# Ordering the expert-weight requests of a hybrid RWKV-7 / Mamba-2 / mixture-of-experts block by their use

## The chip, the cores and the metric

The kernel runs on one core of a Trainium2 chip. The metric is the device time of one execution in microseconds (us). Engines are named as in the profile: PE is TensorE (matmuls), PEld its weight loads, DVE VectorE, ACT ScalarE, POOL GpSimd, SP SyncE. SP does no arithmetic here. It issues DMA transfers, one after the other, and a request that has to wait holds up those behind it on SP.

## The reference, cut to what matters

One block with 512 tokens of 1024 channels in float32: two parallel mixers, an output projection, then a mixture of 32 experts, of which each token uses two. Only the last part is touched here.

```python
D_MODEL = 1024; SEQ = 512; N_GROUPS = 4; EXP_PER_GROUP = 8; N_EXPERTS = 32; TOP_K = 2; D_EXPERT = 512
def run_block(args):            # per expert e, on the tokens routed to it
    tok, e = args
    xb = ht[tok]
    hid = jax.nn.silu(xb @ w_gate[e]) * (xb @ w_up[e])
    return hid @ w_down[e]
...
y = jnp.zeros((T, D), f32).at[buf_tok].add(y_blocks.reshape(-1, D).astype(f32) * buf_w[:, None])
x = x + hier_moe(h2, ...)
return rmsnorm(x, final_norm_g)
```

## The kernel before

Mixers, projection and router fill the first two thirds of the time. Then comes the expert stage. The 32 experts are taken in 16 pairs, and each expert has 64 places for tokens (a loop behind the end handles more than 64; it isn't entered with these inputs). An expert's weights are three matrices of 2 MB (1 MB is 2^20 bytes here): gate, up and down. Each is loaded in two halves of 1 MB, one DMA request each, so a pair of experts takes 12 requests and the stage 192.

**Slots.** A request goes into one of 19 slots of 1 MB. They lie in four pools (tags `wa`, `we`, `wb`, `wc`), and `wslot` hands them out in a ring:

```python
NEXA, NEXB, NEXC, NEXD = 6, 8, 4, 1
def wslot(n, c):
    i = wcount[0] % (NEXA + NEXB + NEXC + NEXD)
    wcount[0] += 1
```

So the request with number r (from 0) waits until weight r - 19 was read for the last time. All requests are issued by SP (L954). A scheduler writes the order of SP, DVE, ACT and POOL, by the order of the program and by which slots it expects to be free; PE's order is that of the program.

**A pair on PE.** In iteration `j` of the main loop:

1. `hidden` for expert 2j: gate and up products, four of the eight 128-row slices of the contraction from the first halves of the weights (L1191, L1192).
2. In its middle, `first`: the hidden rows of pair j - 1 are transposed (`turn`, L1205), the older pair's results are partly added up (`combine`, L1243), and the pair's token selection is transposed (L1179).
3. The second halves of expert 2j's gate and up weights.
4. The scales and the gather's addresses for pair j + 1 (L1141; the gather itself runs on POOL, L1156).
5. `down_both` for pair j - 1 (L1230): the products with the down weights of both its experts.
6. `hidden` for expert 2j + 1, with `second` in its middle: `combine` and the transposes of the gathered tokens (`gather`, L1167).

After the loop come the down products of the last pair, one expert after the other (`down`, L1217), the last `combine`, a final RMS normalization with a gain that ACT loads (L1268, also into a slot of the ring), and the output's writes (L1334).

The down weights of pair j - 1 are thus read after half a pair of gate and up weights of pair j. They are requested, however, with the other weights of their expert: `expert_weights(e)` asks for gate 0, up 0, gate 1, up 1, down 0, down 1 (`WORD`), and is called ahead of each `hidden`.

Of the kernel before, what the change touches and what calls it, by code (L numbers as in the profile page):

```python
# [61 lines left out]
def hybrid_block(ctx: ExitStack, tc: tile.TileContext, a, out):  # L62
    nc = tc.nc
# [3 lines left out]
    def act(o, i, f, **kw):  # L67
        S.activation(o, i, f, **kw)  # L68
# [111 lines left out]
    with tc.tile_pool(name="first", bufs=1) as fp:  # L180
# [31 lines left out]
        for t in range(TT):  # L212
            n = (0, D, 0, D // 2)[t]
# [723 lines left out]
# [3 lines that stand above are left out]
        pool, tg, bf = ((exa, "wa", NEXA) if i < NEXA else (ex, "we", NEXB) if i < NEXA + NEXB else  # L940
                        (exb, "wb", NEXC) if i < NEXA + NEXB + NEXC else (exc, "wc", NEXD))
        return pool.tile([128, n, c], F32, name="we", tag=tg, bufs=bf)

    wsrc = [a["w_exp_gate"][0], a["w_exp_up"][0], a["w_exp_down"][0]]
    WDIM = [(KT, FE), (KT, FE), (4, D)]
    WORD = [(0, 0), (1, 0), (0, 1), (1, 1), (2, 0), (2, 1)]

    def expert_weights(e):
        ws = [[None, None] for j in range(3)]
        for j, i in WORD:  # L950
            n, c = WDIM[j]
            h2 = n // 2
            ws[j][i] = wslot(h2, c)
            nc.sync.dma_start(ws[j][i], wsrc[j][e].rearrange("(p k) f -> p k f", k=n)[:, h2 * i:h2 * i + h2])  # L954
        return ws

    X = mybir.AxisListType.X
    with tc.tile_pool(name="op", bufs=2, side="right") as op:
# [80 lines left out]
        def first(o, v, m, n):  # L1039
            tmp = sm(f"f{n}{o.name}", TT, n)  # L1040
            f = sm(f"g{n}{o.name}", TT)
            V.tensor_tensor(tmp, v, bcast(m, 2, n), op=OP.is_equal)
            V.tensor_tensor(tmp, tmp, bcast(jo[:, 0:n], 1, TT), op=OP.mult)
            V.tensor_reduce(f, tmp, axis=X, op=OP.min)
            V.tensor_tensor(o, bcast(jo[:, 0:n], 1, TT), bcast(f, 2, n), op=OP.is_equal)
# [137 lines left out]


    def hidden(xe, gsl, ws, e, between=lambda: None):
        wg, wu, wd = ws
        lo_, up_ = half[e], half[1 - e]
        pgu = eps_.tile([128, 512], F32, name="pgu", tag="pgu", bufs=2)
        for k in range(KT):
            x = xe[:, k, CAP * e:CAP * e + CAP]  # L1190
            PE.matmul(pgu[lo_], x, wg[k // 4][:, k % 4], start=k == 0, stop=k == KT - 1)  # L1191
            PE.matmul(pgu[up_], x, wu[k // 4][:, k % 4], start=k == 0, stop=k == KT - 1)  # L1192
            if k == KT // 2 - 1:
                between()
        if e == 0:
            hids[0] = mo.tile([128, FE], F32, name="hid", tag="hid")
        hid, g = hids[0], gsl[:, e:e + 1]
        act(hid[up_], pgu[lo_], AF.Silu, scale=g[lo_])
        V.scalar_tensor_tensor(hid[up_], pgu[up_], g[up_], hid[up_], op0=OP.mult, op1=OP.mult)

    def turn(hid, rows=slice(0, 128)):
        pt = eps_.tile([128, 4, 128], F32, name="pt", tag="pt", bufs=1)
        hk = hid.rearrange("p (c k) -> p c k", k=4)
        for k in range(4):
            PE.transpose(pt[:, k, rows], hk[rows, :, k], ident[rows, rows])  # L1205
        if hids[1] is None or rows.start == 0 and rows.stop == 128 or rows.start:
            hids[1] = mo.tile([128, 4, 128], F32, name="hT", tag="hT")
        V.tensor_copy(hids[1][:, :, rows], pt[:, :, rows])
        return hids[1]

    def down(hT, wd, yy, e):
        rows = half[e]
        tags = ("pgu", "pgu") if e == 0 else ("pd0", "pd1")
        pd = [eps_.tile([128, 512], F32, name=f"pd{i}", tag=tags[i], bufs=2 - e) for i in range(2)]
        for k in range(4):
            for i in range(2):
                PE.matmul(pd[i][half[i]], hT[:, k, half[1 - e]], wd[k // 2][:, k % 2, 512 * i:512 * i + 512],  # L1217
                          start=k == 0, stop=k == 3)
        for i in range(2):
            src = pd[i][half[i]]  # L1220
            act(yy[i][rows, 0], src, AF.Copy)
            V.tensor_tensor(yy[i][rows, 1], src, yy[i][rows, 0].bitcast(F32), op=OP.subtract)


    def down_both(hT, wds, yy):
        for i in range(2):
            pd = eps_.tile([128, 512], F32, name=f"pd{i}", tag=f"pd{i}", bufs=1)
            for k in range(4):
                for e in range(2):
                    PE.matmul(pd[half[e]], hT[:, k, half[1 - e]], wds[e][k // 2][:, k % 2, 512 * i:512 * i + 512],  # L1230
                              start=k == 0, stop=k == 3)
            act(yy[i][:, 0], pd, AF.Copy)
            V.tensor_tensor(yy[i][:, 1], pd, yy[i][:, 0].bitcast(F32), op=OP.subtract)

    def result_tiles():
        return [wp.tile([128, 2, 512], F32R, name="yy", tag="raw", bufs=2) for i in range(2)]

    def combine(oT, yy, n, ts=range(TT)):
        for t in ts:
            for i in range(2):  # L1240
                ps = ptile()
                for q in range(2):
                    PE.matmul(ps, oT[0:n, 128 * t:128 * t + 128], yy[i][0:n, q], start=q == 0, stop=q == 1)  # L1243
                av = x2[:, t, 512 * i:512 * i + 512]
                V.tensor_tensor(av, ps, av, op=OP.add)  # L1245
# [19 lines left out]
    def final_gain():  # L1265
        fng = wslot(2, D)[:, 0]
        fn_ = a["final_norm_g"]
        nc.scalar.dma_start(fng, bass.AP(tensor=fn_.tensor, offset=fn_.offset, ap=[[0, 128], [1, D]]))  # L1268
        return fng

    cur = Pair(0)
# [10 lines left out]
    before, older = None, None  # L1282
    NP = NE // 2
    for j in range(NP):
        last = j == NP - 1
        cur.ws = []


        def first():
            if before:  # L1290
                before.hT = turn(before.hid)
            if older:
                combine(older.oT, older.yy, 128, (2, 3))
            if j:
                cur.turned()

        def second():
            if last:
                cur.hT = turn(cur.hid, half[1])
            if before:  # L1300
                combine(before.oT, before.yy, 128, range(4) if last else (0, 1))
            if not last:
                nxt.gather()

        cur.ws.append(expert_weights(2 * j))
        hidden(cur.xe, cur.gsl, cur.ws[0], 0, first)
        cur.hid = hids[0]
        if before:
            if not last:
                nxt = Pair(j + 1)  # L1310
                nxt.scales()
                nxt.fetch()
            before.yy = result_tiles()
            down_both(before.hT, [w[2] for w in before.ws], before.yy)
        cur.ws.append(expert_weights(2 * j + 1))
        hidden(cur.xe, cur.gsl, cur.ws[1], 1, second)
        older, before, cur = before, cur, nxt
    fng = final_gain()
    before.yy = result_tiles()
    down(before.hT, before.ws[0][2], before.yy, 0)  # L1320
    turn(before.hid, half[0])
    down(before.hT, before.ws[1][2], before.yy, 1)

    def final_norm(fng, before=lambda t: None):
        ss = mo.tile([128, TT], F32, name="ss2", tag="ss2")
# [15 lines left out]
    with tc.If(most >= CAP + 1):  # L1341
        sx = mo.tile([128, CAP], F32, name="sx", tag="sx")
        V.tensor_scalar(sx, S0[:, 0], float(CAP), None, op0=OP.add)
        with tc.For_i(0, NE, 1) as e:
            ws = []
            for j in range(3):
                n, c = WDIM[j]
                h2 = n // 2
# [45 lines left out]
```

## Time and profile before

| | |
|---|---|
| runs | 1574.61, 1570.82, 1570.84 us; median 1570.84 |
| the profiled execution | 1568.6 us, of which 1566.9 us are the span that the profile covers |
| PE busy | 1442.3 us (92%) |
| DVE, ACT, POOL busy | 907.1, 662.8, 255.5 us |
| DMA | 325.31 MB, 208 GB/s over the span |
| expert weights | 192 requests of 1024 KB |

The shares are means over stages with different limits. In the expert stage PE and the DMA engines are both near full, so that only the waits and the distances between repeated steps tell which of them sets the pace. Times within the trace count from the span's start.

### The profile page before, as it was taken

How to read it: one execution, taken by the hardware profiler on the slowest of the kernel's cores; microseconds unless marked ns; L12 is line 12 of the kernel's file. 1: busy time of each engine (PE TensorE's matmuls, PEld its weight loads, DVE VectorE, ACT ScalarE, POOL GpSimd, SP SyncE). 2: the span in 40 equal slices, each digit the busy share in tenths (PEclk: the TensorE clock that was granted, in tenths of full speed). 3: DMA queues.
4: the chain of work that ended last, by engine and by line, in shares of the span. 5: the costliest groups of instructions: out<-in, count | busy, mean ns of one | idle time of the engine just before them, and what ended most of it. 6: DMA issues, size and time to landing. Idle time of an engine off the chain costs nothing. (4 is left out here: it accounts for less than half of the span.)

```text
span 1566.9 us, 21550 instructions
## 1 busy us (share of the span) xinstructions
PE 1442.3 (92%) x8066; PEld 933.8 (60%) x8066; DVE 907.1 (58%) x2066; ACT 662.8 (42%) x1278; POOL 255.5 (16%) x240
## 2 busy tenths in 40 slices
PE   6978999899998999989998988899999999999995
PEld 4655676567666777767686766784444344443432
DVE  4698767977778845454565576334444344443434
ACT  6556566566657544546554645321111111111111
POOL 3121002211122000142414355000000000000001
PEclk9998899999999999999999999999999999999998
DMA  4320222212222333774665437877799999999991
GB/s 143 86 66 26 56 85 77 61 57 62 76 63 82 110 94 115 232 210 146 178 187 164 152 101 235 271 283 288 298 419 425 424 424 423 423 424 426 424 419 72
DMA packets 189137, 325.31 MB, mean 208 GB/s; under 512 B 11977, under 2 KB 147395, under 8 KB 163427
## 3 DMA queue, kind: packets, MB, share of 16 engines
q1 hardware_dynamic: 180131, 316.90, 55.8%
q0 software_dynamic: 2304, 4.20, 0.8%
q10 hardware_dynamic: 6592, 2.77, 0.6%
q8 instruction: 66, 1.08, 0.3%
q14 instruction: 44, 0.36, 0.1%
HBM read 306.99 MB, written 21.04 MB: 209 GB/s over the span
## 5 line engine op out<-in xcount | busy, mean ns | idle before, releaser
L149 PE MATMUL pin<-hh,wh 128*128 128x512 f32 x664 | 296.9, 447 | 2.7 <-ACT wh L68 1.5
L151 PE MATMUL pin<-hh,wl 128*128 128x512 f32 x664 | 269.4, 406 | 7.2 <-DVE wl L134 7.2
L150 PE MATMUL pin<-hl,wh 128*128 128x512 f32 x664 | 268.9, 405 | 0.8 <-DVE hl L229 0.8
L1192 PE MATMUL pgu<-we,xe 128*64 128x512 f32 x512 | 233.1, 600 | 7.7 <-DMA we<-in_w_exp_up_dram 7.7
L1191 PE MATMUL pgu<-we,xe 128*64 128x512 f32 x512 | 233.3, 600 | 0.6 <-DMA we<-in_w_exp_gate_dram 0.6
L134 DVE TENSOR_TENSOR wl<-raw,wh 128x1024 fp32r<-128x1024 f32 x115 | 149.6, 1301 | 95.2 <-ACT wh L68 95.2
L68 ACT ACTIVATE wh<-raw 128x1024 fp32r<-128x1024 f32 x115 | 121.5, 1057 | 104.3 <-PE pin L150 84.5
L151 PEld LDWEIGHTS pin<-hh,wl 128*128 128x128 f32 x664 | 128.7, 194 | 41.2 <-DVE wl L134 10.3
L149 PEld LDWEIGHTS pin<-hh,wh 128*128 128x128 f32 x664 | 129.1, 194 | 40.2 <-issue 5.9
L150 PEld LDWEIGHTS pin<-hl,wh 128*128 128x128 f32 x664 | 129.7, 195 | 28.1 <-issue 4.8
L1192 PEld LDWEIGHTS pgu<-we,xe 128*64 128x64 f32 x512 | 67.0, 138 | 79.8 <-issue 62.9
L1191 PEld LDWEIGHTS pgu<-we,xe 128*64 128x64 f32 x512 | 67.0, 138 | 71.5 <-issue 68.1
L1230 PE MATMUL pd<-we,hT 128*64 128x512 f32 x480 | 106.3, 595 | 0.0
L1245 DVE TENSOR_TENSOR x<-gps,x 128x512 f32<-128x512 f32 x128 | 79.3, 683 | 37.8 <-PE gps L1243 37.8
L149 PE MATMUL pin<-yh,wh 128*128 128x512 f32 x192 | 80.7, 420 | 8.8 <-ACT wh L68 3.4
L1156 POOL DMA_INDIRECT xg<-x_d,at x16 | 16.2, 1012 | 420.8 <-DVE oh L1131 373.1
L151 PE MATMUL pin<-yh,wl 128*128 128x512 f32 x192 | 78.0, 406 | 1.1 <-DVE wl L134 1.1
L68 ACT ACT_TABLE_LOAD x54 | 69.3, 1283 | 21.1 <-PE pgu L1192 7.8
L150 PE MATMUL pin<-yl,wh 128*128 128x512 f32 x192 | 77.6, 404 | 0.1
L1243 PE MATMUL gps<-yy,oT 128*128 128x512 f32 x256 | 74.2, 421 | 0.9 <-ACT yy L68 0.7
L1230 PEld LDWEIGHTS pd<-we,hT 128*64 128x64 f32 x480 | 33.2, 137 | 60.8 <-issue 60.5
L68 ACT ACTIVATE yy<-pd 128x512 fp32r<-128x512 f32 (+1 forms) x34 | 20.3, 597 | 109.0 <-PE pd L1230 100.9
(371 smaller groups left out, 2425.5 us busy)
## 6 DMA issues: line engine op xcount, KB each, us to landing
we<-in_w_exp_gate_dram SPq DMA_DIRECT2D x64, 1024.0 KB
we<-in_w_exp_up_dram SPq DMA_DIRECT2D x64, 1024.0 KB
we<-in_w_exp_down_dram SPq DMA_DIRECT2D x64, 1024.0 KB
raw<-in_w_in_dram SPq DMA_DIRECT2D x83, 512.0 KB
lt<-acs_d SPq DMA_DIRECT2D x16, 512.0 KB
raw<-in_w_up_ssd_dram SPq DMA_DIRECT2D x16, 512.0 KB
xc_d<-cv SPq DMA_DIRECT2D x24, 256.0 KB
gt<-g_d SPq DMA_DIRECT2D x24, 256.0 KB
```

The costliest lines, as they stand in the source:

```text
L68: S.activation(o, i, f, **kw)
L134: V.tensor_tensor(lo, raw, hi.bitcast(F32), op=OP.subtract)
L149: PE.matmul(ps, wh[:, k, cs], xh[:, k], start=k == 0, stop=False)
L150: PE.matmul(ps, wh[:, k, cs], xl[:, k], start=False, stop=False)
L151: PE.matmul(ps, wl[:, k, cs], xh[:, k], start=False, stop=k == kt - 1)
L1156: G.indirect_dma_start(out=xg[0:n], out_offset=None, in_=x2_d, in_offset=bass.IndirectOffsetOnAxis(ap=at[0:n, 0:1], axis=0), bounds_check= ...
L1191: PE.matmul(pgu[lo_], x, wg[k // 4][:, k % 4], start=k == 0, stop=k == KT - 1)
L1192: PE.matmul(pgu[up_], x, wu[k // 4][:, k % 4], start=k == 0, stop=k == KT - 1)
L1230: PE.matmul(pd[half[e]], hT[:, k, half[1 - e]], wds[e][k // 2][:, k % 2, 512 * i:512 * i + 512], start=k == 0, stop=k == 3)
L1243: PE.matmul(ps, oT[0:n, 128 * t:128 * t + 128], yy[i][0:n, q], start=q == 0, stop=q == 1)
L1245: V.tensor_tensor(av, ps, av, op=OP.add)
```

## The change

The weights are requested in the order in which PE reads them. `expert_weights` is split into a request for gate and up weights of one expert and one for the down weights of a pair, and the latter is called where `down_both` (after the loop: `down`) needs it: between the gate and up weights of the next pair's two experts. Within a pair's down weights the order is first halves of both experts, then second halves. Number and sizes of the requests, the slots, and all arithmetic stay.

```diff
-    WORD = [(0, 0), (1, 0), (0, 1), (1, 1), (2, 0), (2, 1)]
-
-    def expert_weights(e):
-        ws = [[None, None] for j in range(3)]
-        for j, i in WORD:
+    def weights_of(parts_):
+        ws = {}
+        for e, j, i in parts_:
             n, c = WDIM[j]
             h2 = n // 2
-            ws[j][i] = wslot(h2, c)
-            nc.sync.dma_start(ws[j][i], wsrc[j][e].rearrange("(p k) f -> p k f", k=n)[:, h2 * i:h2 * i + h2])
+            ws[e, j, i] = wslot(h2, c)
+            nc.sync.dma_start(ws[e, j, i], wsrc[j][e].rearrange("(p k) f -> p k f", k=n)[:, h2 * i:h2 * i + h2])
         return ws
+
+    def gate_up_weights(e):
+        ws = weights_of([(e, j, i) for i in range(2) for j in range(2)])
+        return [[ws[e, j, i] for i in range(2)] for j in range(2)]
+
+    def down_weights(p):
+        ws = weights_of([(e, 2, i) for i in range(2) for e in (2 * p, 2 * p + 1)])
+        return [[ws[e, 2, i] for i in range(2)] for e in (2 * p, 2 * p + 1)]
...
-        cur.ws.append(expert_weights(2 * j))
-        hidden(cur.xe, cur.gsl, cur.ws[0], 0, first)
+        hidden(cur.xe, cur.gsl, gate_up_weights(2 * j), 0, first)
...
             before.yy = result_tiles()
-            down_both(before.hT, [w[2] for w in before.ws], before.yy)
-        cur.ws.append(expert_weights(2 * j + 1))
-        hidden(cur.xe, cur.gsl, cur.ws[1], 1, second)
+            down_both(before.hT, down_weights(j - 1), before.yy)
+        hidden(cur.xe, cur.gsl, gate_up_weights(2 * j + 1), 1, second)
         older, before, cur = before, cur, nxt
+    wds = down_weights(NP - 1)
     fng = final_gain()
     before.yy = result_tiles()
-    down(before.hT, before.ws[0][2], before.yy, 0)
+    down(before.hT, wds[0], before.yy, 0)
     turn(before.hid, half[0])
-    down(before.hT, before.ws[1][2], before.yy, 1)
+    down(before.hT, wds[1], before.yy, 1)
```

SP's rows around the 19th request stood like this before; `we` is a weight slot, and the load of `cnt` (the fullest expert's count) is the last row ahead of the requests that reuse a slot:

```order
L954 DMA we<-in_w_exp_gate_dram 128x2048
L1340 TENSOR_LOAD cnt
L1340 ISA x2
L954 DMA we<-in_w_exp_up_dram 128x2048
L954 DMA we<-in_w_exp_gate_dram 128x2048
L954 DMA we<-in_w_exp_up_dram 128x2048
L954 DMA we<-in_w_exp_down_dram 128x2048
L954 DMA we<-in_w_exp_up_dram 128x2048
L954 DMA we<-in_w_exp_gate_dram 128x2048
L954 DMA we<-in_w_exp_up_dram 128x2048
L954 DMA we<-in_w_exp_down_dram 128x2048 x2
```

At the same place on SP stands now:

```order
L954 DMA we<-in_w_exp_down_dram 128x2048 x4
L954 DMA we<-in_w_exp_gate_dram 128x2048
L954 DMA we<-in_w_exp_up_dram 128x2048
L954 DMA we<-in_w_exp_gate_dram 128x2048
L1346 TENSOR_LOAD cnt
L1346 ISA x2
L954 DMA we<-in_w_exp_up_dram 128x2048
L954 DMA we<-in_w_exp_gate_dram 128x2048
L954 DMA we<-in_w_exp_up_dram 128x2048
L954 DMA we<-in_w_exp_gate_dram 128x2048
L954 DMA we<-in_w_exp_up_dram 128x2048
L954 DMA we<-in_w_exp_down_dram 128x2048 x4
```

Before, the row behind the first `down` was an `up` of the next expert: the scheduler had let requests pass one whose slot it expected to be taken. Now the requests stand in the order of the program from the first to the last, four down weights after every eight of gate and up.

The last requests ahead of the output's writes on SP were:

```order
L954 DMA we<-in_w_exp_down_dram 128x2048 x2
L954 DMA we<-in_w_exp_gate_dram 128x2048
L954 DMA we<-in_w_exp_up_dram 128x2048
L954 DMA we<-in_w_exp_gate_dram 128x2048
L954 DMA we<-in_w_exp_up_dram 128x2048
L954 DMA we<-in_w_exp_down_dram 128x2048 x2
L1334 DMA out_dram<-we 128x1024 x4
```

and are now:

```order
L954 DMA we<-in_w_exp_down_dram 128x2048 x4
L954 DMA we<-in_w_exp_gate_dram 128x2048
L954 DMA we<-in_w_exp_up_dram 128x2048
L954 DMA we<-in_w_exp_gate_dram 128x2048
L954 DMA we<-in_w_exp_up_dram 128x2048
L954 DMA we<-in_w_exp_down_dram 128x2048 x4
L1340 DMA out_dram<-we 128x1024 x4
```

Four down weights, those of experts 30 and 31, follow the last gate and up weights, where two did. PE, DVE and POOL keep their order. On ACT one row moves; near the end of its list the load of the final gain stood ahead of the last activation of `hid`:

```order
L68 ACTIVATE yy<-pd_12207 128x512
L68 ACTIVATE yy<-pd_12218 128x512
L1268 DMA we<-in_final_norm_g_dram 128x1024
L68 ACTIVATE hid<-pgu,gsl 64x512
L68 ACTIVATE yy<-pd_12303 64x512
```

and stands behind it now:

```order
L68 ACTIVATE yy<-pd_12203 128x512
L68 ACTIVATE yy<-pd_12214 128x512
L68 ACTIVATE hid<-pgu,gsl 64x512
L1276 DMA we<-in_final_norm_g_dram 128x1024
L68 ACTIVATE yy<-pd_12303 64x512
```

## Rows read from the trace of the kernel before

**Rows 1.** The page: the span, and GB/s moved in 40 equal slices.
```profile
span 1566.9 us, 21550 instructions
...
GB/s 143 86 66 26 56 85 77 61 57 62 76 63 82 110 94 115 232 210 146 178 187 164 152 101 235 271 283 288 298 419 425 424 424 423 423 424 426 424 419 72
```

**Rows 2.** Timeline of PE, turns of pairs 2, 3, 4, 15 (start, us, what).
```profile
1118.01 0.74 PE L1205 MATMUL pt<-ident,hid 128*128 128x128 f32 x4
...
1146.71 0.75 PE L1205 MATMUL pt<-ident,hid 128*128 128x128 f32 x4
...
1175.41 0.75 PE L1205 MATMUL pt<-ident,hid 128*128 128x128 f32 x4
...
1510.55 0.74 PE L1205 MATMUL pt<-ident,hid 128*128 128x128 f32 x4
```

**Rows 3.** Windows: length; busy PE, PEld, DVE, ACT, POOL; PEclk; DMA share; GB/s.
```profile
1076.63:1080.00 3.37, 3.37 (x18) 1.11 (x16) 0.00 (x0) 0.00 (x0) 0.00 (x0) 1.00 0.67 224
1098.00:1104.00 6.00, 6.00 (x30) 2.01 (x28) 2.56 (x8) 0.60 (x1) 0.99 (x1) 1.00 0.31 74
1118.00:1146.70 28.70, 28.70 (x138) 12.23 (x136) 12.78 (x33) 4.52 (x9) 0.99 (x1) 1.00 0.85 340
1146.70:1175.40 28.70, 28.70 (x138) 12.23 (x136) 12.78 (x33) 4.52 (x9) 0.99 (x1) 1.00 1.01 423
1265.80:1510.50 244.70, 238.35 (x1089) 99.10 (x1088) 101.07 (x258) 36.18 (x72) 7.94 (x8) 1.00 1.01 424
1527.00:1529.00 2.00, 2.00 (x11) 1.09 (x8) 0.42 (x1) 0.00 (x0) 0.00 (x0) 1.00 0.76 313
```

**Rows 4.** Timeline of PE, first half of expert 30 ([idle before <- releaser]).
```profile
1505.38 1.02 PE L1191 MATMUL pgu<-we,xe 128*64 128x512 f32 x2
1506.97 0.64 PE L1192 MATMUL pgu<-we,xe 128*64 128x512 f32 x1 [0.57 <-DMA we<-in_w_exp_up_dram]
```

**Rows 5.** Waits of PE, 1066 to 1567 (us in total, times, longest).
```profile
PE pgu L1192 <- DMA we<-in_w_exp_up_dram: 7.7, 10, 1.4
...
PE pgu L1191 <- DMA we<-in_w_exp_gate_dram: 0.6, 1, 0.6
```

**Rows 6.** Waits of SP's queue, the whole span.
```profile
SPq L954 <- PE pd L1230: 138.8, 26, 19.5
```

**Rows 7.** Timeline of SP, requests around the first reuse of slots.
```profile
1061.31 0.33 SPq L954 DMA_DIRECT2D we<-in_w_exp_gate_dram  x1
1076.63 0.33 SPq L954 DMA_DIRECT2D we<-in_w_exp_up_dram  x1
...
1080.07 0.33 SPq L954 DMA_DIRECT2D we<-in_w_exp_up_dram  x1
...
1088.59 14.32 SPq L954 DMA_DIRECT2D we<-in_w_exp_down_dram  x2
```

**Rows 8.** Timeline of PE, gather of pair 1 to second half of expert 3.
```profile
1083.40 1.16 PE L1167 MATMUL gps<-ident,xg 128*128 128x128 f32 x8
...
1092.62 0.64 PE L1191 MATMUL pgu<-we,xe 128*64 128x512 f32 x1
...
1097.19 7.09 PE L1230 MATMUL pd<-we,hT 128*64 128x512 f32 x32
...
1110.99 0.64 PE L1191 MATMUL pgu<-we,xe 128*64 128x512 f32 x1
```

**Rows 9.** Timelines of PE, ACT and DVE in the last pair and after it.
```profile
1517.35 7.04 PE L1230 MATMUL pd<-we,hT 128*64 128x512 f32 x32
...
1532.94 0.64 PE L1191 MATMUL pgu<-we,xe 128*64 128x512 f32 x1
...
1524.75 0.35 ACTq L1268 DMA_DIRECT2D we<-in_final_norm_g_dram  x1
1536.64 0.69 ACT L68 ACTIVATE hid<-pgu,gsl 64x512 f32<-64x512 f32 x1 [11.55 <-PE pgu L1192]
...
1552.14 1.28 DVE L1333 SCALAR_TENSOR_TENSOR we<-x,ss,we 128x1024 f32<-128x1024 f32 x1 [0.37 <-POOL ss L1332]
```

More of the change, by code (lines that the diff above doesn't have):

```diff
@@ L1185, in hidden @@
     def hidden(xe, gsl, ws, e, between=lambda: None):
-        wg, wu, wd = ws
+        wg, wu = ws[:2]
         lo_, up_ = half[e], half[1 - e]
@@ L1285, in hybrid_block @@
         last = j == NP - 1
-        cur.ws = []
         def first():
```

## Prediction, made before the changed kernel ran

> **What bounds the kernel now.** First the page: the 16 DMA engines move 424 GB/s in the last quarter of the span and far less in the slices before it [rows 1]. The last quarter is the expert stage; the change touches nothing else, and no engine but SP and ACT gets another order.
>
> Second, the turn matmuls (L1205), one set per pair of experts, as a stopwatch on TensorE. From pair 2 to 3 and from 3 to 4 a pair takes 28.70 us (1118.01, 1146.71, 1175.41), and then 335.14 us for the eleven pairs up to pair 15 at 1510.55 [rows 2]: 30.47 each. Third, why: in the windows table the first of these pairs ran at 340 GB/s and the second at 423, both in 28.70 us with TensorE busy throughout, while from 1265.8 to 1510.5 TensorE was busy 238.35 of 244.70 us at 424 GB/s [rows 3]. A pair is 12 requests of 1 MB (2^20 bytes), which take 12 x 1.0486 / 0.424 = 29.68 us, or 2.473 us each. TensorE alone needs 28.70 us, the stream 29.68: once the prefetched lead is used up, the stream sets the pace. Fourth, where it waits: nearly always at the first up weights of a pair, as at 1506.97 [rows 4]; the waits table names the same line [rows 5]. The idle time there (7.7 us) counts only what lies past the modelled end of running matmuls; in rows 4 the gap between two starts that otherwise follow at once is 1506.97 - 1505.38 = 1.59 us. I therefore size the loss by pairs: 335.14 - 11 x 28.70 = **19.44 us**.
>
> Fifth, why the lead is used up. Nineteen slots of 1 MB stand full when TensorE starts. A slot is reused in ring order, so request r waits until weight r - 19 was read. SP waited 138.8 us for the release by down matmuls [rows 6]: two down requests held the queue 14.32 us from 1088.59 on, with all later ones behind them [rows 7]. Expert 0's down weights sat in slots 4 and 5 although they are read only after half of expert 2. Meanwhile the stream fell to 74 GB/s [rows 3]. It ends at about 1528.5, for 1527 to 1529 still moved 313 GB/s: 1.48 us of full rate [rows 3].
>
> **What the change does, part by part.**
>
> *Requests.* 192 before and after, of the same size, and SP's issue costs stay the same. The first 19 go out at the same places, the last at 1061.31 [rows 7], with four down weights instead of six among them: pair 0's, as requests 12 to 15, not read before 1097.19 [rows 8], 36 us after the last of the 19. Cost 0.
>
> *Stream.* Each slot is now freed in the order of the ring. I count requests as freed and served. TensorE frees two slots after each half of an expert and four towards the end of both downs. In the first pairs SP's requests show the releases: at 1076.63 and 1080.07 [rows 7], each frees two slots. Then [rows 8]: expert 1's first half ends with the gather, 1083.4; its second half and the first of expert 2, 3.4 us each, at 1087.9 and 1091.4; the half from 1092.62 at 1096.1; the downs from 1097.19 free two slots after three quarters, 1102.4, and two at the end, 1104.1; the next halves end at 1107.6 and 1114.4. The restart at 1076.63 moved 224 GB/s over 3.37 us [rows 3], 0.674 MB short of full rate, which is 1.6 us. So the n-th new request is served by 1078.2 + 2.473 n. At each release the sum freed before against the sum served is 2 to 0.7 (1080), 4 to 2.1, 6 to 3.9, 8 to 5.3, 10 to 7.2, 12 to 9.8, 14 to 10.5, 16 to 11.9, 18 to 14.6: never empty, with at least 1.3 requests (3.2 us) in hand. Later TensorE frees faster than the stream serves (28.70 against 29.68), so the surplus grows. The stream should run full from 1078 and end at 1078.2 + 173 x 2.473 = 1506, some 22 us earlier.
>
> *TensorE.* If it never waits, pair 15 turns at 1118.01 + 13 x 28.70 = 1491.1. Its weights: the first up of expert 30 is request 177, there at 1078.2 + 159 x 2.473 = 1471.4, needed 3.5 us before the turn, 1487.6: 16 us spare. The last down weight of pair 14 is request 183, there at 1486.2. The downs start 6.8 us after the turn (1517.35 - 1510.55), and it is read 1.7 us later, at 1499.6 [rows 9]: **13.4 us spare**, the least of all places. Second gate and up halves of expert 31 (187): 1496.1 against 1513.5. Last (191): 1506, and no down weight of this pair is read before 1517, for the hid activation before it moves from 1536.64 [rows 9] to 1517.2. The spare was largest at the start and falls by 0.98 us a pair. All of the 19.44 us come back, and the stream stays hidden under TensorE.
>
> *New waits.* All requests past the nineteenth now wait for TensorE, more often and for less. Behind a waiting request stand only later ones on SP, and, at the end, the output's writes. On ACT the load of the final gain moves behind one hid activation, from 1524.75 to after 1536.64 in old time [rows 9]. Its issue takes 0.35 us, behind an activation of 0.69; it is read first at 1552.14. Both places move by the same 19.44 us, and the 14 us between them must hold 512 KB, whose full-rate price is 1.2 us. Cost 0. Were it to come late, the four normalizations would wait behind it.
>
> *Another shape of the same price.* One restart costs 1.6 us. If the stream ran empty once in a pair, it would lose 13.75 x 1.6 = 22 us by request 183; the spare takes 13.4 of it and 8.6 remain, a gain of 10.8. Full cover to one restart a pair bounds the term: 19.4 to 10.8 us. I take full cover, as the count above never reached zero.
>
> *Sum.* On the profiled execution (1568.6 us for a span of 1566.9) 1568.6 - 19.4 = 1549.2. The runs' median lies 2.2 us higher, at 1570.84; if those 2.2 us are the stream's, they vanish as well, if not they stay (1551.4). I take 1550.3.
>
> **Rivals.**
>
> *The stream does not start earlier, only the order helps* (something other than ring order holds it until 1140). It still ends at 1528.5; behind the first up weights of expert 30 stand 14 requests instead of 10, so these come 4 x 2.473 = 9.9 us sooner: 1558.7. The same size comes out if only the shown idle returns (7.7 + 0.6): 1560.3. For it: the idle column. Against: 28.70 us at 423 GB/s, and the one long SP wait.
>
> *Nothing changes*: the extra 1.6 us a pair would be TensorE's own pace. The two undisturbed pairs, with the same instructions, speak against it: 1568.6.
>
> *Slower: the stream runs empty at every other release.* Each request now goes out only when TensorE frees a slot, two at a time; a stream that is fed so could restart again and again. At two restarts a pair it loses 44 us by request 183, less 13.4 spare = 30.6 us in place of 19.4: 1579.8. It decides from (19.4 + 13.4) / (13.75 x 1.6) = 1.5 restarts a pair. Against it: the surplus counted above. The Trainium skill ("DMA: Bandwidth & Descriptors", section "Bandwidth") bears on it: its table (transfers issued from GpSimd) gives a single one of 1 MB 341 GB/s and only one of 16 MB 425. By 341 GB/s for every request, weight 183 would come at 1585 and the kernel at about 1635 us, an estimate from that page. The trace disagrees for requests that overlap: 424 GB/s in the same 1 MB pieces over 245 us [rows 3].
>
> **How the numbers follow.** 0.3% is 4.7 us, about the least that can be told from no change. Forecast (1546 to 1555) 0.80; partial gain (1555 to 1563) 0.13; nothing 0.03; slower 0.04. Both gains are faster by over 0.3%: 0.93, within it 0.03, slower 0.04. The range, 1546 to 1559, takes the forecast and the first half of the partial gain.
>
> **What would show it.** Right: turns 28.7 us apart up to pair 15, near 1491; no wait of pgu for up weights; over 400 GB/s from 1080 on and a stream that ends near 1506; SP's waits for pd replaced by shorter ones for pgu. Then TensorE alone bounds the stage. Wrong: windows below 400 GB/s between 1080 and 1140, or turns still 30 us apart. Under 411 GB/s on average the spare of 13.4 us is gone; at 393 the gain is.

## The result, and the profile after

The change takes 1555.74 us (median of 5 runs, 1552.31 to 1560.87), beside 1572.47 us for the kernel before on the same chip: ratio 0.989, 95% interval 0.9867 to 0.9913. The profiled execution is one of 1552.31 us. It is 16.3 us faster than the one before (1568.6); the sum had 19.4. The page:

```profile
span 1550.6 us, 21648 instructions
...
GB/s 135 97 62 31 58 85 67 60 70 49 84 64 77 103 102 109 211 211 163 148 218 150 159 108 164 286 305 212 424 424 426 423 424 424 423 425 424 424 423 140
...
q0 software_dynamic: 2304, 4.20, 0.7%
```

The rate stands at 424 GB/s already in the slice that held 298 in [rows 1]. The third row is POOL's DMA queue (packets, MB, share); it comes back below. The stopwatch, turns of pairs 2, 3, 4 and 15 on PE (the line is now L1213):

```profile
1120.68 0.75 PE L1213 MATMUL pt<-ident,hid 128*128 128x128 f32 x4
...
1149.39 0.75 PE L1213 MATMUL pt<-ident,hid 128*128 128x128 f32 x4
...
1178.10 0.74 PE L1213 MATMUL pt<-ident,hid 128*128 128x128 f32 x4
...
1493.81 0.75 PE L1213 MATMUL pt<-ident,hid 128*128 128x128 f32 x4
```

From 1120.68 to 1493.81 the 13 pairs take 373.13 us, 28.70 each, the last as the first. Before, they took 392.54 [rows 2]. That is 19.41 us less, beside a forecast of 19.44. The windows that answer to [rows 3]:

```profile
1076.63:1080.00 3.37, 3.37 (x16) 0.97 (x14) 0.00 (x0) 0.00 (x0) 0.00 (x0) 0.86 0.12 45
1098.00:1104.00 6.00, 6.00 (x34) 2.52 (x32) 2.55 (x12) 1.12 (x2) 0.99 (x1) 1.00 1.01 421
1118.00:1146.70 28.70, 28.69 (x138) 12.23 (x136) 12.77 (x33) 4.51 (x10) 0.99 (x1) 1.00 1.01 426
...
1265.80:1510.50 244.70, 244.70 (x1158) 104.44 (x1158) 105.45 (x265) 38.65 (x76) 7.94 (x8) 1.00 1.01 424
```

Where 74 GB/s were moved, 421 are, and PE is busy for all of the last 244.70 us. (The first window is low since the whole stage begins some 2.7 us later here: SP's request of 1076.63 [rows 7] now goes out at 1079.30.) PE's waits from 1066 on, all that take over 0.5 us in one go on a transfer:

```profile
PE gps L1175 <- DMA xg<-x_d,at: 1.4, 1, 1.4
```

It is the gather of the first pair's tokens. No wait for weights is left of [rows 5]. SP's waits for PE, for [rows 6]:

```profile
SPq L954 <- PE pgu L1200: 58.4, 16, 12.4
...
SPq L954 <- PE pd L1238: 31.1, 12, 5.4
```

The longest is the very first, 12.4 us, while all 19 slots stand full. Those for down products fell from 138.8 to 31.1 us.

**Where the other 3.1 us are.** The forecast's 19.44 us came back as 19.41 up to turn 15. From there to the end of the span it is 56.79 us, beside 56.35 before: 0.44 lost. And turn 2 came at 1120.68 in place of 1118.01: 2.67 us later, ahead of anything that the change can save. 19.41 - 0.44 - 2.67 = 16.30. To keep what lies ahead apart, the experiments compare **the stage**, from the turn of pair 1 to the span's end: before 1566.9 - 1091.51 = 475.4 us, with the change 1550.6 - 1094.18 = 456.4.

One step of the prediction doesn't fit: the stream of weights should have ended near 1506, or 1508.7 with the 2.67. Windows of the change at its end:

```profile
1513.00:1514.00 1.00, 1.00 (x6) 0.57 (x4) 1.00 (x2) 0.00 (x0) 0.00 (x0) 1.00 0.95 401
1517.00:1518.00 1.00, 1.00 (x7) 0.29 (x4) 0.73 (x2) 0.00 (x0) 0.00 (x0) 1.00 0.70 295
1519.00:1520.00 1.00, 1.00 (x8) 0.28 (x4) 0.00 (x0) 0.00 (x0) 0.00 (x0) 1.00 0.33 139
1520.00:1521.00 1.00, 1.00 (x4) 0.14 (x1) 0.00 (x0) 0.64 (x1) 0.00 (x0) 1.00 0.10 41
```

The last weights move at 1521, 12.3 us behind the forecast, and the rate falls over the last 7 us instead of at once. So the mechanism is there, but the spare of 13.4 us may not be. The experiments ask how much there is.

### The profile page after: what moved, and what is told of

Same layout as the page of the kernel before. It is cut to its first block, busy times and chain, and to the rows that moved or that the text cites. A ratio compares the mean times of both kernels' runs of the same rounds, so it can differ in the third digit from the quotient of the medians.

```text
span 1550.6 us, 21648 instructions
## 1 busy us (share of the span) xinstructions
PE 1430.4 (92%) x8066; PEld 931.9 (60%) x8066; DVE 909.3 (59%) x2066; ACT 662.0 (43%) x1278; POOL 254.6 (16%) x240
```

## The experiments

The stages, in us (span less the turn of pair 1; each from one profile; e1, e2, f1, f2 and g3 ran only once):

| | span | turn of pair 1 | stage | against the change |
|---|---|---|---|---|
| before; profiled again (h1) | 1566.9; 1566.4 | 1091.51; 1091.96 | 475.4; 474.4 | +18.3 (mean) |
| the change; again (f4) | 1550.6; 1552.9 | 1094.18; 1096.17 | 456.4; 456.7 | mean 456.6 |
| e1: 14 slots | 1557.0 | 1087.58 | 469.4 | +12.8 |
| e2: 11 slots | 1561.5 | 1082.38 | 479.1 | +22.5 |
| e3: downs behind their own pair | 1560.5 | 1094.96 | 465.5 | +9.0 |
| e4: old order, two rings | 1567.7 | 1101.13 | 466.6 | +10.0 |
| f1: 14 slots, no gathers | 1545.9 | 1087.60 | 458.3 | +1.7 |
| f2: half the additions | 1548.7 | 1091.95 | 456.8 | +0.2 |
| g3: half the additions, no gathers | 1539.6 | 1094.53 | 445.1 | -11.5 |

**e1 and e2: fewer slots.** A slot less means that the stream starts one request, 2.473 us, later against PE. This uses up the spare.

```diff
-    NEXA, NEXB, NEXC, NEXD = 6, 8, 4, 1
+    NEXA, NEXB, NEXC, NEXD = 1, 8, 4, 1      # e1; e2: 1, 8, 1, 1
```

> The changed order with 14 slots instead of 19 (the first pool has 1 slot instead of 6); nothing else differs. Clock of the stage: from the turn of pair 1 to the end of the span, 456.4 us in the changed kernel's profile, 475.4 before. Theory (the stream runs full from the first release, TensorE paces the stage, 13.4 us to spare): five slots fewer make every weight 5 x 2.473 = 12.4 us later against TensorE, so 1.0 us of the spare is left; turns stay 28.70 us apart and the stage takes 456 to 458 us. Rival (the gain comes from the order of arrival alone, the lead does not matter): the same. Rival (the stream runs empty between releases and the spare is much smaller than counted): TensorE waits, stage 465 us or more.

> The changed order with 11 slots (pools of 1, 8, 1, 1). Theory: eight slots fewer make every weight 19.8 us later; the last down weight of pair 14 then comes 6.4 us after TensorE wants it, the first up of expert 30 3.6 us after. The first pairs stay at 28.70 us, the last few lengthen towards 29.7, and the stage takes 456.4 + 6.4 = about 463 us. Rival (only the order of arrival counts): 456 to 458, as with 19 slots. Rival (stream runs empty between releases): well over 470.

Both missed. e1 took 1558.74 us, e2 1563.17. PE's waits for weights in e1:

```profile
PE pd L1238 <- DMA we<-in_w_exp_down_dram: 1.9, 4, 1.1
PE pgu L1200 <- DMA we<-in_w_exp_up_dram: 1.0, 1, 1.0
```

Pairs run at 28.70 us up to turn 9 and at 29.5 to 31.8 after it. Five requests later are 5 x 2.473 = 12.4 us, and the stage lost 12.8: all of it, so the spare is about zero. In e2 eight requests are 19.8 us and 22.5 are lost; the 2.7 us beyond were not followed up.

**e3 and e4: parts of the change.** e3 asks for a pair's down weights behind the gate and up weights of the same pair, in one ring. e4 leaves the order of before and gives the down weights a ring of their own (8 slots; 11 for gate and up), so that they don't hold the others' slots.

```diff
 e3, on the change
-        hidden(cur.xe, cur.gsl, gate_up_weights(2 * j + 1), 1, second)
+        gu = gate_up_weights(2 * j + 1)
+        cur.wds = down_weights(j)
+        hidden(cur.xe, cur.gsl, gu, 1, second)
...
 e4, on the kernel before
-    def wslot(n, c):
-        i = wcount[0] % (NEXA + NEXB + NEXC + NEXD)
+    def wslot(n, c, down=0):
+        i = wcount[down] % (8 if down else 11)
...
```

> The changed kernel, but a pair's down weights are requested right behind the gate and up weights of the same pair, ahead of the next pair's first expert (half a pair earlier than they are read). Theory: the four slots of pair 0's down weights (requests 8 to 11) hold up requests 27 to 30 until about 1102 to 1104 in time of before, when the stream has served all earlier ones by 1098; that costs one stop of some 6 us, after which the first up of expert 30 arrives 0.4 us before it is wanted. Stage 456 to 459 us, that is 16 to 19 us less than before, though the order is not that of use. Rival (what counts is that weights arrive in the order of their use): the first up of a pair has four down weights ahead of it as before, so the waits come back, at 1.6 us a pair from pair 4 on: stage 465 to 475 us.

> The kernel before with its old order of requests, but the down weights have a ring of their own of 8 slots and gate and up one of 11 (19 together, as before); a down weight that waits for its slot no longer holds slots of the other ring, but still stands ahead of later requests on SP. Theory (the gain is the stream's lost time between 1090 and 1140, which came from slots held by down weights): the stream stops once, for 3 to 5 us around 1101, ends near 1510, and the first up of expert 30 comes some 2 us before it is wanted: stage 456 to 460 us with the old order of requests. Rival (the order of arrival is what gains): stage 470 to 476 us, as before.

e3: 1564.26 us, ratio to before 0.9962 (0.9941 to 0.9983). e4: 1561.24 us, 0.9948 (0.9922 to 0.9973). Both gain, less than expected; the rivals' stages (465 to 475, 470 to 476) are nearer. Windows of e3, then of e4; the last of each begins with the first request that reuses a slot and is 130 us long:

```profile
1105.00:1110.00 5.00, 5.00 (x26) 1.71 (x24) 1.36 (x2) 0.60 (x1) 0.00 (x0) 1.00 0.99 369
1120.00:1140.00 20.00, 19.99 (x97) 8.11 (x94) 8.24 (x24) 2.47 (x4) 0.99 (x1) 1.00 0.99 406
1080.09:1210.09 130.00, 129.99 (x620) 54.56 (x616) 53.33 (x137) 22.17 (x43) 3.97 (x4) 1.00 1.00 411
```

```profile
1105.00:1110.00 5.00, 5.00 (x30) 2.17 (x28) 2.55 (x12) 0.68 (x1) 0.99 (x1) 1.00 1.01 416
1110.00:1120.00 10.00, 10.00 (x49) 4.06 (x45) 3.35 (x6) 1.19 (x2) 0.00 (x0) 1.00 0.82 303
1120.00:1140.00 20.00, 20.00 (x99) 8.61 (x100) 9.52 (x29) 3.92 (x8) 0.99 (x1) 1.00 1.01 427
1086.26:1216.26 130.00, 130.00 (x620) 54.56 (x616) 53.34 (x137) 22.15 (x43) 3.95 (x4) 1.00 0.99 409
```

The same 130 us before and with the change:

```profile
1076.63:1206.63 130.00, 130.00 (x619) 55.44 (x616) 53.16 (x137) 22.19 (x43) 3.97 (x4) 1.00 0.93 380
```

```profile
1079.30:1209.30 130.00, 129.99 (x620) 54.57 (x616) 53.30 (x137) 22.17 (x43) 3.97 (x4) 1.00 1.00 418
```

In e3 and e4 the stops are shorter, but not gone: e4 still has one between 1110 and 1120 (303 GB/s). Beside the change's 418 GB/s, the stream lacks 130 x 38 / 424 = 11.7 us before, 2.1 in e3 and 2.8 in e4. The stages are longer than the change's by 18.3, 9.0 and 10.0 us, so 6.6 to 7.2 us are left in all three.

They are what is common to the three: the up weights stand four requests deeper in the stream, and PE waits for them (in e4 from turn 9 on, 3.5 us in 5 waits). Four requests are 4 x 2.473 = 9.9 us for the first up weights; with the change, however, the last down weights of a pair bind, for which the prediction had counted 13.4 us spare in place of 16, and that leaves some 7. So of some 18.3 us the stops are worth about 11 and the order of arrival about 7. This split is worked out from the windows; no run has the old order without any stop.

**f1, f2 and g3: what the spare is, and what ate it.** f2 leaves out half of the additions of the older pair's results in 14 pairs. PE is busy with them for 2.36 us a pair, 33 in all; the pairs come 28.70 - 26.51 = 2.19 us closer, 31 in all. What PE can gain by this is the stream's spare. f1 leaves out the gathers of pairs 2 to 15, which run on POOL's DMA queue, in e1. g3 leaves out both. All three leave out part of the computation.

```diff
 f1 and g3
-                nxt.fetch()
 f2 and g3
-            if older:
-                combine(older.oT, older.yy, 128, (2, 3))
```

> The change with 14 slots as in e1, and without the gathers of pairs 2 to 15 (the tokens of pair 1 are used again, so the outputs differ). It leaves 14 x 2 gathers out of the DMA engines' work, nothing of PE's. Theory A (the gathers' bytes run on the same 16 engines and cost the weight stream about 0.62 us a pair, so that a pair needs 30.3 us and not 29.68): pairs that waited take 29.7 us in place of 30.3 to 31.8, and the stage from the turn of pair 1 to the end, 469.4 us in e1, is about 8.7 us shorter, 460 to 462. Theory B (the gathers cost the stream nothing; the spare is missing for another reason): 468 to 470, as e1.

> The change without half of the additions of the older pair's results (2.36 us of PE in each of 14 pairs, 33 us in all; the outputs differ). It asks how much spare the stream has left behind PE. By the prediction's count (13.4 us spare at the last down weights of pair 14) the stage from the turn of pair 1 to the end, 456.4 us with the change, would be 13.4 us shorter, about 443, before PE waits for weights. By the corrected count (the spare is 0.2 us, since the gathers take 8.7 us of the stream's time and a weight can be read only 3.8 us after its place in the byte stream) PE waits nearly at once for what it saves, and the stage is 455 to 457; a pair then takes 30.3 us with waits from the first ones whose lead is used up.

> The change without the gathers of pairs 2 to 15 and without half of the additions of results (both leave outputs out). It measures the spare that the stream has without gathers. In f2, with gathers, the 33 us that PE saved gave nothing: spare 0. In f1 the gathers were worth 11.1 us against e1 (8.7 by their bytes). Corrected count: the spare is now 8.7 to 11.1 us, so the stage is 456.7 less that, 445.5 to 448; what then still lacks to the prediction's count of 13.4 (443) is the lag between a weight's place in the byte stream and its use. If gathers and lag do not add up in this way, the stage is 455 to 457, as f2, or 443.

f2, turns of pairs 7 to 10, and PE's waits for weights:

```profile
1250.96 0.75 PE L1213 MATMUL pt<-ident,hid 128*128 128x128 f32 x4
...
1277.47 0.75 PE L1213 MATMUL pt<-ident,hid 128*128 128x128 f32 x4
...
1305.52 0.74 PE L1213 MATMUL pt<-ident,hid 128*128 128x128 f32 x4
...
1336.29 0.75 PE L1213 MATMUL pt<-ident,hid 128*128 128x128 f32 x4
```

```profile
PE pd L1238 <- DMA we<-in_w_exp_down_dram: 15.5, 16, 1.5
```

A pair takes 26.51 us of PE, until the lead is used up after pair 8; then 30.77, 30.28, 30.66, 30.47, 30.19 and 30.11, 30.41 in the mean, with the waits at the down weights, where the prediction had put the least spare. The stage is as long as with the change: 31 us less of PE's time are worth nothing, and the spare is zero within the 1 us by which stages repeat. Without the gathers (g3) the same edit gains 11.5 us, so the spare is 11.5. The gathers of 14 pairs thus take 456.75 - 445.07 = 11.7 us of the stream's lead, 0.83 each. With 14 slots they took 469.42 - 458.30 = 11.1 (e1, f1). Their bytes alone, 4.20 MB / 16 = 0.262 MB each, would be 0.62 us at 424 GB/s, 8.7 in all: that part of the expectation was too small. Where the rest comes from is seen at the ends of the streams; f2, then g3:

```profile
1511.00:1512.00 1.00, 1.00 (x5) 0.43 (x4) 1.00 (x3) 0.00 (x0) 0.00 (x0) 1.00 0.87 369
1515.00:1516.00 1.00, 1.00 (x6) 0.29 (x4) 0.41 (x1) 0.00 (x0) 0.00 (x0) 1.00 0.62 262
1518.00:1519.00 1.00, 0.84 (x2) 0.00 (x0) 0.25 (x1) 0.68 (x1) 0.00 (x0) 1.00 0.08 33
```

```profile
1506.00:1507.00 1.00, 1.00 (x6) 0.29 (x4) 0.75 (x2) 0.00 (x0) 0.00 (x0) 1.00 1.03 434
1507.00:1508.00 1.00, 1.00 (x8) 0.41 (x6) 0.00 (x0) 0.00 (x0) 0.00 (x0) 1.00 0.76 320
1510.00:1511.00 1.00, 0.30 (x3) 0.11 (x4) 0.74 (x1) 0.06 (x1) 0.00 (x0) 1.00 0.62 164
```

With gathers the rate falls over 8 us (1511 to 1519), without them over some 4 (1507 to 1511, the last row with the final gain's load, issued at 1509.67). The traces also hold the times at which the sixteen increments of each weight's semaphore arrive. For the last down weight of pair 14 the last of them comes 9.0 us behind the first with the change and in f2, 3.6 in g3; behind the mean of the sixteen it comes 3.65 us with the change and 1.65 in g3. The parts of a weight thus come in far apart, and further with the gathers. With the change the last part is there at 1502.70, and PE's weight load starts on it:

```profile
1502.74 0.19 PEld L1238 LDWEIGHTS pd<-we,hT 128*64 128x64 f32 x3 [0.28 <-DMA we<-in_w_exp_down_dram]
```

The forecast had it at 1486.2, or 1488.9 with the 2.67: it is 13.8 us late, as much as the spare of 13.4. In g3, where pair 1 turns 3.02 us later than before, it is there at 1491.72 and 2.5 us late. So the gathers delay it by 11.3 us, of which 8.7 are their bytes and 2.0 the parts that lie further apart; 0.6 stay open. Which engine is late the records don't tell.

**f3, g1, g2: slots that come later.** From the request of the output projection's first weights to the router's logits e1 and e2 took 73.2 and 76.1 us, the change 82.7. f3 keeps 19 slots, only nine of them free early; g1 also holds requests 16 to 18 back until the first gather has landed.

```diff
 f3, g1, g2
-    NEXA, NEXB, NEXC, NEXD = 6, 8, 4, 1
+    NEXA, NEXB, NEXC, NEXD = 1, 8, 9, 1
...
 g1
+            if gate is not None:
+                G.tensor_copy(ws[e, j, i][0:1, 0, 0:1], gate)
...
```

> The change with 19 slots as before, of which only 9 (not 14) stand outside the memory that the mixers' tensors leave free; 10 come free with it. e1 and e2, with 9 early slots, reached the logits 8 to 11 us sooner after the first load of the output projection. Theory A (weights that are loaded ahead take DMA time from the output projection's own loads): the part ahead of the stage is 8 to 10 us shorter, the stage's stream starts with fewer weights loaded but still runs full from the 19th on; the stage itself 456 to 462; in all 1541 to 1552 and below the change. Theory B (the 8 to 11 us were variation of the granted clock): within 0.3% of the change, or slower, up to 1562, since five weights fewer stand loaded when TensorE starts.

> f3 with the last three of the ten late slots (requests 16 to 18) held back until the tokens of the first pair have landed (one element of the gathered tile is copied into slot 16, so the request waits for it). In f3 the logits came 12 us sooner than with the change alone, but the first gather, issued at 1060.1 behind some ten weights, landed at 1068.1, and PE waited 8.8 us for it. Theory A (the gather waits behind the weights in the DMA engines): that wait falls to 1 to 2 us, the turn of pair 1 comes 6 to 8 us earlier than in f3 (1089.8), at 1082 to 1084, the stage stays at 456 to 460 us, and the whole is 4 to 8 us below f3. Theory B (the wait has another cause): wait and time as in f3.

> f3 once more, on the same chip as g1: PE waits 8 to 9 us for the first gather, and the median is within 0.3% of the first one's place relative to the kernel before, 0.990.

f3: 1553.78 us, ratio to before 0.9899 (0.9881 to 0.9917). g1: 1555.1 us, 0.9898 (0.9869 to 0.9927). g2: 1556.04 us, 0.9906 (0.9874 to 0.9938). None can be told from the change. The logits did come sooner (1043.09 in f3, 1055.70 with the change), but the first gather, issued behind the ten late weights, of which two to three were still to come, was late. Timelines, first f3's on POOL (the issue), then f3's on PE (the first use), then g1's on PE:

```profile
1060.11 1.31 POOL L1164 DMA_INDIRECT xg<-x_d,at  x1 [17.18 <-DVE oh L1139]
```

```profile
1068.07 1.97 PE L1175 MATMUL gps<-ident,xg 128*128 128x128 f32 x8 [8.84 <-DMA xg<-x_d,at]
```

```profile
1065.91 1.97 PE L1183 MATMUL gps<-ident,xg 128*128 128x128 f32 x8 [4.39 <-DMA xg<-x_d,at]
```

It takes 8.0 us from issue to use in f3 and 9.15 in g2 (1062.70 to 1071.85); in g1, issued at 1062.19, 3.7. So the gather did wait for weights that were still coming in. In the profiles the turn of pair 1 comes 6.2 us sooner in g1 than in g2 (1088.31, 1094.47), less than hoped for, as the gather's addresses were no earlier, and the stage lost 1.2 of it. The medians of the runs, 0.9 us apart with some 10 us between a kernel's own runs, don't show it.

**f4 and h1: change and kernel before once more.**

> The change once more, on the same chip as f3. If the sum of 19.4 us for the stage is right and what came late ahead of the stage in the first profile (2.7 us) is variation, the stage from the turn of pair 1 to the end is again 456 to 457 us, and the median lies 15 to 20 us below that of the kernel before. If the 2.7 us belong to the change, the part ahead of the stage is again later by that much.

> The kernel before once more, profiled a second time. Its stage from the turn of pair 1 to the end took 475.4 us, and the turn came at 1091.5; with the change 456.4 and 456.7 us, and turns at 1094.2 and 1096.2. If the stage's length is what the order of requests sets and the part ahead of it varies from execution to execution, the stage is 475 to 476 again and the turn lies anywhere from 1091 to 1097. If the later turn belongs to the change, the turn is at 1091 to 1092 again.

f4: 1553.76 us, beside 1568.57 before, 0.989 (0.9865 to 0.9916); stage 456.7. h1: 1569.9 us; stage 474.4. The stages repeat within 1 us and differ by 18.3. The turn of pair 1 came at 1091.51 and 1091.96 before, at 1094.18 and 1096.17 with the change. f2 and g3, with the same requests ahead of it, had it at 1091.95 and 1094.53. So the two overlap, but the runs' medians gain 14.8 to 16.7 us where the stage gains 18.3. Whether the change costs 2 to 3 us ahead of the stage stays open.

## Why the prediction was right, and which step was not

*What bounds the kernel* was right: a stream of weights behind which PE waits, because a few down weights held the ring. With the request order changed, the stop of [rows 3] is gone and the stage gains 17.7 to 19.0 us, beside the term of 19.44.

*Stream and TensorE* hold the step that failed: "The stream should run full from 1078 and end at 1078.2 + 173 x 2.473 = 1506", and from it "13.4 us spare". The first half is right (406 GB/s from 1080 to 1100, 420 to 427 in the windows of 20 us after it). The end is not: the size was taken as if all of the 424 GB/s were weights. The gathers of the next pair's tokens move in the same windows. Measured, they cost 11.7 of the 13.4 us, and some 2 are lost otherwise (13.4 less the 11.5 of g3): a weight can be read only when its last part has come, which even without gathers is 1.65 us behind the mean of its parts. The price stood in the rows from the start: a pair took 30.47 us where twelve requests were worked out to 29.68. These 0.79 us a pair were passed over; over 13.75 pairs they are 10.9 us. (The first of those eleven pairs still took 28.89 us, turn at 1204.30; the ten behind it took 30.6 each, 0.9 more than worked out.) The Trainium skill says that DMAs issued from GpSimd run on the same 16 engines of the core ("DMA: Bandwidth & Descriptors", section "SWDGE vs HWDGE vs iDMA"); f2 and g3 agree, with 0.83 us a gather.

So "the stream stays hidden under TensorE" holds by a hair. The sum came out because the spare ended at zero and not below; that is luck, as the count had not shown it. The cost of one more late request would have been its full 2.473 us, as e1 shows.

*Another shape of the same price*, one restart a pair (10.8 us), did not occur, nor did the slower rival: none of the 20 us windows between 1080 and 1480 is under 406 GB/s. *Only the order helps* (9.9 us) did not happen as such, but the order has a price: the 7 us that e3 and e4 lack beyond their stops. *New waits*: SP waits as said; the final gain's load, at 1520.65 behind the hid activation, delayed nothing that the waits show.

*Sum*: 1550.3 forecast, 1555.74 and 1553.76 measured; the first lies just inside the band called a partial gain. From turn 2 to turn 15 the first profiles give 19.41 us, the second ones (h1, f4) 391.63 - 373.09 = 18.54: the match to 0.03 us is closer than the profiles repeat. On the profiled execution 3.1 us are lacking (1552.31 beside 1549.2), ahead of turn 2 (2.67) and behind turn 15 (0.44). The median lies another 3.4 us higher, where the sum had left 1.1.

## What to carry to other kernels

Where requests share a ring of slots, ask for data in the order of their last use: a request whose data are used late keeps its slot from all that follow, and one that stands early in the stream delays all behind it; here the stops were worth some 11 us and the place in the stream some 7, and e4, which cured most of the stops alone, gained less than half. Count every transfer that runs beside a stream, the small ones too: if a steady step takes longer than its own bytes at the observed rate (30.47 against 29.68 us), look for what else moves on the same engines. And a spare is best measured by shortening the other side: when 31 us less of PE's time gain nothing, the stream is the next bound, and only less traffic gives more (g3).

## What the runs showed of the hardware that was not expected

A gather of 0.262 MB costs the stream 0.83 us, a third more than its bytes at 424 GB/s (0.62). With gathers the stream's rate falls over 7 to 8 us at its end, without them over 4, and the sixteen increments of one weight spread over 9.0 us there, without them over 3.6. The Trainium skill ("DMA: Bandwidth & Descriptors", section "Why a DMA increments its semaphore by 16 and not by 1") says that data have landed only when every engine that took part has reported; PE's weight load at 1502.74, behind a last increment at 1502.70, agrees; no run here tells which engine an increment is from.

A gather that needs 3.7 us from issue to use takes 8.0 to 9.2 while weights come in; of the change's sixteen gathers the median from issue to landing is 8.1. The Trainium skill ("DMA: Bandwidth & Descriptors", section "Queues, rings and completion order") says that each engine takes turns between its queues, packet by packet; by that rule one would expect so small a transfer not to wait for all of what was queued before it. No run here shows such turns: in f3 it came at 1068.07, about when the queued weights were done: 367 GB/s from 1060 to 1068, 47 from 1068 to 1075.
